# Attention latents in alternating PSUM banks, and an output projection of seven block products

## Chip, core and metric

One core of a Trainium2 chip runs the kernel. The metric is device time in microseconds (us), lower is better. Five engines run side by side, each with its own queue in order: TensorE (PE; its weight loads are shown as PEld), VectorE (DVE), ScalarE (ACT), GpSimd (POOL) and SyncE (SP), which issues the DMAs. Matmuls write to PSUM, in banks of 512 float32 columns; operands lie in SBUF.

## The reference

A mixer block on 2048 latent tokens of 1024 features, with 256 context tokens. Cut to what matters here:

```python
u = h @ w_in[l]                                  # h: normed, modulated x
q, k, v = _mla_qkv(u, ...)                       # 4 heads, low-rank q and kv
attn = _attend(q, k_all, v_all)                  # 2048 queries, 2304 keys
y = _branches(u, attn, w_pool[l], pool_scale[l]) @ w_out[l]
x_new = x + gate[:, None, :] * y
# _branches: concat([silu(gate_a) * attn, silu(gate_p) * pooled])
```

## The kernel before

Every float32 operand of a matmul is split into a high and a low part, and a product is three matmuls: high by high, high by low, low by high. `split` (lines 96 to 100) copies the high part on ScalarE and subtracts on VectorE (or GpSimd).

**Attention.** There are 16 blocks (4 heads by 4 groups of 512 queries), each of two halves p of 256 queries. `scores(p, i)` computes 128 queries by 2304 keys in five chunks: four of 512 columns in banks "A" (5 of them) and one of 256 in a bank "X" (2 of them); VectorE takes the maxima, ScalarE the exponentials (line 795) and VectorE transposes 32x32 blocks (line 798). `shuffle(p)` issues 16 DMAs on SP that bring the blocks into place. `pv(p)` then works in nine steps: a step makes the high half on ScalarE (line 855) and the low half on GpSimd, or for one step on VectorE (line 857), and six products (line 823) sum into the block's bank "O", of which there is one. The steps of `pv` follow the scores at some 28 score steps' distance, written out in `attn`.

At a block's end `norm` transposes the sums' reciprocals in a bank X, `latents` splits bank O into two SBUF tiles, and `finish`, called at the fourth step of the next half, multiplies these by the value weights (line 912, in a bank X), by the gate (line 914) and stores to `brd`. The gate is multiplied by the reciprocals on GpSimd before (line 895). The last half, `pv_last`, transposes on TensorE (line 841) instead of by DMA; the order at the end is 28, 29, 31, 30.

**Output projection.** `load_wo` loads w_out in four pieces of 256 rows after the shuffles of p = 28, 29, 30 and at the end; `out_weights` splits them (lines 933 and 935) at the steps that WO_AT lists. Then for each of eight pairs of token tiles (t2): 8 x 256 columns of `brd` are loaded (line 1028), split, and multiplied in four banks of 24 products each (2 token tiles by 2 halves of the output columns; 8 row tiles by 3). VectorE multiplies each bank by the gate (line 1060), GpSimd adds x (line 1063; VectorE in the last token tile), and SP stores. The last bank is computed in two halves of 256 columns.

The scheduler of the framework orders the instructions of each engine by program order and by when their operands and buffers are free; `order(a, b)` adds an edge, and buffers of a tag ("B": 8, "M": 6, "T": 10, "W": 5) are handed out as they come free.

Of the kernel before, what the change touches and what calls it, by code (L numbers as in the profile page):

```python
# [17 lines left out]
H = 4  # L18
# [41 lines left out]
WO_AT = (1, 5, 11, 12, 12, 12, 13, 13)  # L60
# [5 lines left out]
def tile_hybrid_block(ctx: ExitStack, tc: tile.TileContext, x, c, cx, c_ctx, w_mod, b_mod, norm_g,  # L66
# [23 lines left out]
    def pt(tag, cols=512):  # L90
        return ps.tile([128, cols], F32, tag=tag, bufs=PBUFS[tag], name=nm("p" + tag))
# [346 lines left out]
    def tok(hf, k):  # L438
# [112 lines left out]
        tk = ps.tile([128, H, 128], F16, tag="X", bufs=PBUFS["X"], name=nm("pX"))  # L551
# [251 lines left out]
    PT, pool_last = {}, []  # L803
# [15 lines left out]
    def pv_mm(p, o, j2, t):  # L819
        for jj in range(2):  # L820
            j = 2 * j2 + jj
            for m, (a, c) in enumerate(((0, 0), (1, 0), (0, 1))):
                nc.tensor.matmul(o, lhsT=V[0][:, j, a], rhs=t[:, c, jj], start=(j == 0 and m == 0),  # L823
                                 stop=(j == NJ - 1 and m == 2))
# [22 lines left out]
    def pv(p):  # L847
        o = out_bank(p)
        src = PT.pop(p).rearrange("p q i j b -> p (q i) j b")
        ts = []  # L850

        def halves(j2):
            t = st("M", [2, 2, 8, 32], F16)
            s2 = src[:, :, 2 * j2:2 * j2 + 2, :].rearrange("p x j b -> p j x b")
            nc.scalar.activation(out=t[:, 0], in_=s2, func=AF.Copy)  # L855
            eng = nc.vector if j2 == 4 or (p == NP - 2 and j2 % 2) else nc.gpsimd
            lo = eng.tensor_tensor(out=t[:, 1], in0=s2, in1=t[:, 0], op=ALU.subtract)  # L857
            if eng is nc.gpsimd:
                pool_last.append(lo.ins)
            ts.append(t)  # L860

        for j2 in range(NJ // 2):
            if j2 == 0:
                halves(0)
                halves(1)
            if j2 + 2 < NJ // 2:
                halves(j2 + 2)
            t = ts.pop(0)
            pv_mm(p, o, j2, t)
            yield  # L870

    def norm(n):
# [6 lines left out]
        b = pt("X")  # L879
# [21 lines left out]
    def latents(n):  # L901

        o = O.pop(n)
        ol = [st("T", [512], F32R) for _ in range(2)]
        split(o, *ol)
        return ol

    def finish(n, ol, gau):
        h, qb = blocks[n]
        b = pt("X")  # L910
        for m, (a, c) in enumerate(((0, 0), (1, 0), (0, 1))):
            nc.tensor.matmul(b, lhsT=wuv[0][:, a, h * 128:(h + 1) * 128], rhs=ol[c], start=(m == 0), stop=(m == 2))  # L912
# [6 lines left out]
    wo = []  # L919

    wraw, tail = [], []

    def load_wo(k2):
        raw = st("B", [2, D])
        nc.sync.dma_start(out=raw, in_=w_out[k2 * 256:(k2 + 1) * 256, :].rearrange("(k p) n -> p k n", p=128))
        wraw.append(raw)

    def out_weights():
        for raw in wraw:
            w = st("W", [2, 2, D], F32R)  # L930
            wo.append(w)
            for k in range(2):
                a = nc.scalar.activation(out=w[:, 0, k], in_=raw[:, k], func=AF.Copy)
                order(tail[-1], a.ins, "the last block of attention comes first")
                nc.vector.tensor_tensor(out=w[:, 1, k], in0=raw[:, k], in1=w[:, 0, k].bitcast(F32), op=ALU.subtract)
                yield

    def pv_all():
# [11 lines left out]
        gr_ = norm(NP // 2 - 1)  # L950
        for k, _ in enumerate(pv_last(NP - 1)):
            if k == 3:
                finish(NP // 2 - 2, ol, gate_norm(*gaus))
            yield
        gau = gate_norm(*gr_)
        yield from pv(NP - 2)
        finish(NP // 2 - 1, latents(NP // 2 - 1), gau)

    PER = 10
    WO_PF = (28, 29, 30)  # L960
    pg = pv_all()

    def attn():

        done = 0
        for p in range(NP):
# [12 lines left out]
            if p == NP - 1:  # L979
                load_wo(3)  # L980
                return
            with tc.issue_after(shuffle(p)):
                if h < H and p % 8 in K_PF:
                    load_k(h, (K_PF.index(p % 8),))
                if p in WO_PF:
                    load_wo(WO_PF.index(p))

# [27 lines left out]
    ow = out_weights()  # L1015
    for n, _ in enumerate(pg):
        for _ in range(WO_AT.count(n)):
            next(ow)
    for _ in ow:
# [3 lines left out]
    gb = st("M", [D])  # L1023
    nc.sync.dma_start(out=gb, in_=gated.partition_broadcast(128))
    for t2 in range(8):
        t0 = t2 * HB
        br = st("B", [8, HB])
        nc.sync.dma_start(out=br, in_=brd[:, :, :, t0:t0 + HB].rearrange("a h p n -> p (a h) n"))
        bh, bl = st("B", [8, HB], F32R), st("B", [8, HB], F32R)
        split(br, bh, bl)  # L1030
        bank = {}

        def mm(k, n, ks, c0=0, c1=512):
            if (k, n, c0) not in bank:
                bank[k, n, c0] = pt("A")
            for kt in ks:
                w = wo[kt // 2]
                for m, (a, c) in enumerate(((bh, 0), (bh, 1), (bl, 0))):
                    nc.tensor.matmul(bank[k, n, c0][:, 0:c1 - c0], lhsT=a[:, kt, k * 128:(k + 1) * 128],  # L1039
                                     rhs=w[:, c, kt % 2, n * 512 + c0:n * 512 + c1],  # L1040
                                     start=(kt == 0 and m == 0), stop=(kt == 7 and m == 2))

        for ks in [range(8)] if t2 else [(2 * i, 2 * i + 1) for i in range(4)]:
            for k in range(2):
                for n in range(2):
                    if t2 == 7 and k == 1 and n == 1:
                        mm(k, n, ks, 0, 256)
                        mm(k, n, ks, 256, 512)
                    else:
                        mm(k, n, ks)  # L1050
        for k in range(2):
            xr = st("M", [D])
            rows = slice(t0 + k * 128, t0 + (k + 1) * 128)
            nc.sync.dma_start(out=xr, in_=x[rows, :])
            last = t2 == 7 and k == 1
            for n in range(2):
                for c0, c1 in ((0, 256), (256, 512)) if last and n == 1 else ((0, 512),):
                    nsl = slice(n * 512 + c0, n * 512 + c1)
                    o = st("T", [512])
                    nc.vector.tensor_tensor(out=o[:, 0:c1 - c0], in0=bank[k, n, c0][:, 0:c1 - c0], in1=gb[:, nsl],  # L1060
                                            op=ALU.mult)
                    eng = nc.vector if last else nc.gpsimd
                    eng.tensor_tensor(out=xr[:, nsl], in0=o[:, 0:c1 - c0], in1=xr[:, nsl], op=ALU.add)  # L1063
                    if last:
                        nc.sync.dma_start(out=out[rows, nsl], in_=xr[:, nsl])
            if not last:
                nc.sync.dma_start(out=out[rows, :], in_=xr)
# [48 lines left out]
```

## Time and profile before

| | us |
|---|---|
| median of 3 runs | 1268.37 (1267.26 to 1270.73) |
| profiled execution | 1265.99 |
| span of the profiled execution | 1264.2 |
| TensorE busy | 1208.2 (96%) |
| VectorE busy | 832.2 (66%) |
| ScalarE busy | 733.5 (58%) |
| GpSimd busy | 565.7 (45%) |

Busy time is the sum of an engine's instructions in the profile; matmuls overlap, so their durations are longer than the distance from one to the next. A line number is that of the kernel before. "Idle before, releaser" tells how long an engine stood before an instruction and which instruction of which engine ended that.

### The profile page before, as it was taken

The page shows a single profiled execution, that of the slowest core. Times are in us where ns is not written, and L with a number is a line of the kernel's source. Part 1 is how long each engine was busy: PE and PEld are TensorE (multiplying, and loading weights), DVE is VectorE, ACT ScalarE, POOL GpSimd, SP SyncE. Part 2 cuts the span into 40 slices and gives each one's busy share as a digit, 9 for nine tenths or more (in the row PEclk, how much of TensorE's full clock was granted, in tenths as well). Part 3 has the DMA queues.
Part 4 walks back from the last instruction along what each step waited for, and adds up shares of the span by engine and source line. Part 5 has one row for each costly group of instructions (what it writes and reads, how often), then busy time and mean ns, then how long its engine had stood idle before and what let it go on. Part 6 is the DMA issues. An engine that isn't in the chain of part 4 may idle for free.

```text
span 1264.2 us, 22297 instructions
## 1 busy us (share of the span) xinstructions
PE 1208.2 (96%) x7805; PEld 949.8 (75%) x7805; DVE 832.2 (66%) x1595; ACT 733.5 (58%) x1780; POOL 565.7 (45%) x638
## 2 busy tenths in 40 slices
PE   6899999999999999899999999999999999999998
PEld 2698989989899999665666566666665666788887
DVE  4876654756556555579888888888888876732211
ACT  5585655645675654367777777777777777510000
POOL 3645313525344343024566656555655574342221
PEclk9799999999999999999999999999999999999999
DMA  9546942485336646457897788878877888664321
GB/s 305 150 130 139 231 124 70 123 189 176 88 81 143 164 111 169 124 129 179 220 221 174 176 207 202 190 178 212 196 177 178 187 198 245 201 219 145 118 83 50
DMA packets 208213, 208.66 MB, mean 165 GB/s; under 512 B 92339, under 2 KB 168420, under 8 KB 207974
## 3 DMA queue, kind: packets, MB, share of 16 engines
q1 hardware_dynamic: 208102, 207.25, 63.3%
q8 instruction: 61, 1.00, 0.3%
q14 instruction: 50, 0.41, 0.1%
HBM read 98.50 MB, written 35.56 MB: 106 GB/s over the span
## 4 chain that ended last, share of the span: by engine, by line
PE 75%; DMA 9%; DVE 6%; ACT 5%; SPq 3%; issue 2%; POOL 1%; ACTq 0%; DVEq 0%; POOLq 0%
PE pA L590 17%; PE pA L774 17%; PE pA L1039 13%; PE pO L823 10%; PE pA L246 6%; DMA W<-W 2%; PE pA L521 2%; PE pX L774 2%; ACT T L795 2%; DVE W L798 2%; DMA M<-in_w_in_dram 2%; SPq L813 1%; PE pX L912 1%; DVE mx L777 1%; DMA qrd<-U 1%
## 5 line engine op out<-in xcount | busy, mean ns | idle before, releaser
L857 POOL TENSOR_TENSOR M<-W,M 128x512 f16<-128x512 f32 x244 | 291.5, 1219 | 239.1 <-ACT M L855 187.7
L590 PE MATMUL pA<-W,B 128*128 128x256 f32 x2304 | 306.4, 286 | 0.1
L774 PE MATMUL pA<-B,M 128*128 128x512 f16 x1280 | 298.1, 379 | 8.5 <-ACT T L795 6.1
L590 PEld LDWEIGHTS pA<-W,B 128*128 128x128 f32 x2304 | 289.2, 191 | 3.5 <-issue 0.9
L774 PEld LDWEIGHTS <-M 128*128 128x128 f16 x1600 | 154.7, 98 | 153.3 <-issue 13.9
L798 DVE STREAM_TRANSPOSE W<-T 128x512 f32<-128x512 f32 x310 | 194.1, 643 | 58.5 <-ACT T L795 44.6
L855 ACT ACTIVATE M<-W 128x512 f16<-128x512 f32 x279 | 162.2, 633 | 107.6 <-PE pO L823 95.0
L823 PE MATMUL pO<-M,B 128*128 128x256 f16 x1728 | 219.7, 273 | 3.0 <-POOL M L857 1.8
L823 PEld LDWEIGHTS <-B 128*128 128x128 f16 x1728 | 167.6, 98 | 48.1 <-issue 11.2
L795 ACT ACTIVATE T<-pA,nm,gm 128x512 f32<-128x512 f32 x248 | 189.3, 773 | 7.8 <-DVE nm L783 6.3
L1039 PE MATMUL pA<-W,B 128*128 128x512 f32 (+1 forms) x792 | 177.8, 384 | 1.7 <-ACT B L98 1.7
L777 DVE TENSOR_REDUCE mx<-pA 128x1 f32<-128x512 f32 x256 | 168.3, 671 | 11.5 <-PE pA L774 11.2
L1039 PEld LDWEIGHTS pA<-W,B 128*128 128x128 f32 x792 | 144.7, 188 | 30.8 <-ACT B L98 1.9
L1063 POOL TENSOR_TENSOR M<-T,M 128x512 f32<-128x512 f32 x30 | 40.7, 1361 | 110.9 <-DVE T L1060 106.7
L1060 DVE TENSOR_TENSOR T<-pA,M 128x512 f32<-128x512 f32 (+1 forms) x33 | 22.0, 672 | 100.6 <-PE pA L1039 100.6
L246 PE MATMUL pA<-B,W 128*128 128x448 f32 (+1 forms) x288 | 86.6, 372 | 0.0
L98 ACT ACTIVATE B<-M 128x1024 fp32r<-128x1024 f32 (+2 forms) x53 | 55.2, 1043 | 43.3 <-DMA M<-in_w_in_dram 37.4
L99 DVE TENSOR_TENSOR B<-M,B 128x1024 fp32r<-128x1024 f32 x48 | 59.8, 1247 | 30.9 <-ACT B L98 30.9
L98 ACT ACTIVATE B<-B 128x2048 fp32r<-128x2048 f32 x8 | 15.3, 1914 | 77.4 <-DMA B<-brd 77.4
L246 PEld LDWEIGHTS pA<-B,W 128*128 128x128 f32 x288 | 54.7, 197 | 4.4 <-DVE T L275 0.9
L246 PE MATMUL pA<-W,W 128*128 128x448 f32 (+1 forms) x144 | 52.9, 369 | 0.0
L795 ACT ACTIVATION_READ_ACCUMULATOR T<-pA,nm,gm 128x1 f32 x248 | 49.5, 200 | 0.0
(193 smaller groups left out, 1500.8 us busy)
## 6 DMA issues: line engine op xcount, KB each, us to landing
W<-W SPq DMA_DIRECT2D x496, 144.0 KB
M<-in_w_in_dram SPq DMA_DIRECT2D x48, 512.0 KB
B<-in_x_dram SPq DMA_DIRECT2D x16, 512.0 KB
B<-brd SPq DMA_DIRECT2D x8, 1024.0 KB
M<-in_x_dram SPq DMA_DIRECT2D x16, 512.0 KB
out_dram<-M SPq DMA_DIRECT2D x15, 512.0 KB
brd<-T SPq DMA_DIRECT2D x24, 256.0 KB
kd<-T SPq DMA_DIRECT2D x36, 128.0 KB
```

The lines of the kernel that those rows point to most:

```text
L98: a = nc.scalar.activation(out=hi, in_=src, func=AF.Copy)
L99: (eng or nc.vector).tensor_tensor(out=lo, in0=src, in1=hi if hi.dtype == F16 else hi.bitcast(F32), op=ALU.subtract)
L246: nc.tensor.matmul(p[:, c0:NTOK], lhsT=a[:, kt, k * 128:(k + 1) * 128], rhs=b, start=(kt == 0 and n == 0), stop=(kt == KT - 1 and n == 2))
L590: nc.tensor.matmul(p[:, i * HB:(i + 1) * HB], lhsT=w[:, a, kt, :], rhs=b[:, kt, :], start=(m == 0), stop=(m == 23))
L774: nc.tensor.matmul(b[:, s0:s0 + sn], lhsT=q[:, a, c, p % 2, i], rhs=kt[ki][:, kc, o:o + sn], start=(m == 0), stop=(m == 4))
L777: nc.vector.reduce_max(mx[:, n:n + 1], b[:, :w], axis=AX.X)
L795: nc.scalar.activation(out=e[:, :w], in_=sp[n][:, :w], func=AF.Exp, bias=ng, scale=escale, accum_out=rs[:, n:n + 1])
L798: nc.vector.transpose(TP[p][:, :, i, j0:j1, :].rearrange("p q j b -> p j q b"), e[:, :w].rearrange("p (j q b) -> p j q b", q=4, b=32))
L823: nc.tensor.matmul(o, lhsT=V[0][:, j, a], rhs=t[:, c, jj], start=(j == 0 and m == 0), stop=(j == NJ - 1 and m == 2))
L855: nc.scalar.activation(out=t[:, 0], in_=s2, func=AF.Copy)
L857: lo = eng.tensor_tensor(out=t[:, 1], in0=s2, in1=t[:, 0], op=ALU.subtract)
L1039: nc.tensor.matmul(bank[k, n, c0][:, 0:c1 - c0], lhsT=a[:, kt, k * 128:(k + 1) * 128], rhs=w[:, c, kt % 2, n * 512 + c0:n * 512 + c1], sta ...
```

## The change

**Banks.** A block's products go to bank O for even blocks and to a bank X for odd ones; `norm` uses the other of the two. `finish` writes its product into the bank that `latents` has just read, and an edge puts it behind the products of the next block that stand before it in the program.

**Projection.** Token tiles are taken in pairs as before. For the first pair (t2 = 0) four banks are computed from eight block products (`plain_pair`), each of 128 tokens by 512 features by 512 columns. For the other seven, the 2x2 blocks A (tokens by features) and B (features by columns) are multiplied by the form of Strassen and Winograd with seven block products, with sums S1 to S4 of the blocks of A, and T1 to T4 of the blocks of B. The sums are made on VectorE before the operands are split. The products are summed on VectorE as they leave PSUM, and the gate and x are applied on GpSimd in two operations (on VectorE for the last block). The second pair (t2 = 1) takes its products in another order, those without T1 to T4 first.

**Loads.** w_out is loaded in four blocks of 512 rows by 512 columns, after the shuffles of p = 26 to 29; the first pair's `brd` and x are loaded after that of p = 30, and the gate before the last steps of attention. WO_AT is spread over more steps.

The core of the diff:

```diff
-WO_AT = (1, 5, 11, 12, 12, 12, 13, 13)
+WO_AT = (1, 4, 7, 10, 13, 15, 17, 18)
+BR_AT = 16
@@ out_bank, norm, finish
-            O[p // 2] = pt("O")
+            O[p // 2] = pt("OX"[p // 2 % 2])
-        b = pt("X")
+        b = pt("XO"[n % 2])
     def finish(n, ol, gau):
-        b = pt("X")
+        ol, b = ol
         for m, (a, c) in enumerate(((0, 0), (1, 0), (0, 1))):
+            i = nc.tensor.matmul(b, lhsT=wuv[0][:, a, h * 128:(h + 1) * 128], rhs=ol[c], ...)
+            order(pv_done[-1], i.ins, "products of the next block come first")
@@ weights
+    def wo_sums():
+        def wo_sum(out, a, b, op):
+            for k in (0, 2):
+                i = nc.vector.tensor_tensor(out=out[:, k:k + 2], in0=a[:, k:k + 2], in1=b[:, k:k + 2], op=op)
+                order(op_last[3], i.ins, "the first operands come first")
+        b00, b01, b10, b11 = (wraw.pop((a, b)) for a in range(2) for b in range(2))
+        t1, t2 = st("B", [4, 512]), st("B", [4, 512])
+        wo_sum(t1, b01, b00, ALU.subtract)
+        wo_sum(b01, b11, b01, ALU.subtract)
+        yield
+        wo_sum(t2, b01, b00, ALU.add)
+        yield from wo_pair("T2", t2, "W")
+        wo_sum(t2, b10, t2, ALU.subtract)
+        yield from wo_pair("T1", t1, "B")
+        yield from wo_pair("T3", b01, "B")
+        yield from wo_pair("T4", t2, "W")
@@ projection
+    FORM = ((1, "A00", "B00"), (6, "S2", "T2"), (5, "S1", "T1"), (7, "S3", "T3"), (2, "A01", "B10"),
+            (3, "S4", "B11"), (4, "A11", "T4"))
+    def close(t2, xr, k, n, o, c0=0, c1=512, ops=(ALU.mult, ALU.add)):
+        last = t2 == 7 and (k, n) == (1, 0)
+        eng = nc.vector if last else nc.gpsimd
+        ...
+    def products(b, c, w, first, last_, c0=0, c1=512, kts=range(4)):
+        for kt in kts:
+            for m, (x0, x1) in enumerate(((0, 0), (0, 1), (1, 0))):
+                nc.tensor.matmul(b[:, c0:c1], lhsT=c[:, x0, kt, :], rhs=w[x1][:, kt, c0:c1], ...)
+    def operand(src):
+        c = st("M", [2, 4, 128], F32R)
+        nc.scalar.activation(out=c[:, 0], in_=src, func=AF.Copy)
+        op_last.append(nc.vector.tensor_tensor(out=c[:, 1], in0=src, in1=c[:, 0].bitcast(F32), op=ALU.subtract).ins)
+        return c
+    def sums_of(br):
+        for key, a, b, op in (("S1", "A10", "A11", ALU.add), ("S2", "S1", "A00", ALU.subtract),
+                              ("S3", "A00", "A10", ALU.subtract), ("S4", "A01", "S2", ALU.subtract)):
+            ...
+            nc.vector.tensor_tensor(out=v[key], in0=v[a], in1=v[b], op=op)
+    def out_pair(t2, v, xr, early={}):
+        for i, a, b in (FORM if t2 > 1 else [FORM[j] for j in (0, 4, 5, 1, 2, 3, 6)]):
+            c = early.pop(a, None) or operand(v[a])
+            pb = pt("A")
+            products(pb, c, wo[b], True, True, ...)      # 12 matmuls
+            if i == 1:
+                p1 = st("T", [512])
+                nc.scalar.copy(out=p1, in_=pb)
+            elif i == 6:
+                u = add(pb, p1)                          # VectorE, PSUM + SBUF
+            elif i == 5:
+                z = add(pb, u)
+            elif i == 7:
+                close(t2, xr, 1, 1, add(pb, z))
+                y = add(pb, u)
+            ...
@@ order of the projection
+    sums = wo_sums()
+    for n, _ in enumerate(first):                        # plain_pair(0), eight steps
+        if n == 0:
+            br, xr = load_pair(1)
+        if n < 3:
+            next(sums, None)
+        elif n == 3:
+            early["A00"], early["A01"] = (operand(blocks_of(br)[key]) for key in ("A00", "A01"))
+            v = sums_of(br)
+        elif n == 5:
+            early["S4"] = operand(v["S4"])
+        else:
+            next(sums, None)
+    for _ in sums:
+        pass
+    for t2 in range(1, 8):
+        for n, _ in enumerate(out_pair(t2, v, xr, early)):
+            if n == 1 and t2 < 7:
+                br, nxr = load_pair(t2 + 1)
+            if n == 3 and t2 < 7:
+                nv = sums_of(br)
```

## Rows read from the trace of the kernel before

**Rows 1.** The page: busy us, share of the span and instructions of each engine.
```profile
PE 1208.2 (96%) x7805; PEld 949.8 (75%) x7805; DVE 832.2 (66%) x1595; ACT 733.5 (58%) x1780; POOL 565.7 (45%) x638
```

**Rows 2.** Stretches: length, busy PE, PEld, DVE, ACT, POOL, clock, DMA share, GB/s.
```profile
556.00:1050.00 494.00, 477.27 (x3083) 302.58 (x3083) 413.71 (x849) 365.95 (x865) 295.13 (x247) 1.00 0.79 191
...
1066.00:1070.00 4.00, 3.09 (x21) 2.23 (x22) 3.93 (x8) 4.00 (x8) 0.00 (x0) 1.00 1.01 408
...
174.00:179.00 5.00, 2.92 (x22) 2.41 (x21) 4.21 (x8) 2.76 (x6) 0.52 (x1) 1.00 0.00 0
179.00:183.00 4.00, 4.00 (x19) 3.62 (x18) 1.90 (x5) 1.67 (x4) 0.19 (x1) 0.57 0.33 77
```

**Rows 3.** TensorE's waits, 340 to 1050 us: releaser, us, times, longest.
```profile
PE pX L912 <- ACT T L98: 9.0, 13, 0.7
```

**Rows 4.** Timeline at block changes (start, us, engine, line, instruction): TensorE, GpSimd.
```profile
634.28 0.73 PE L912 MATMUL pX<-T,M 128*128 128x512 f32 x2 [0.69 <-ACT T L98]
...
869.65 0.82 PE L823 MATMUL pO<-M,B 128*128 128x256 f16 x6
871.16 0.73 PE L912 MATMUL pX<-T,M 128*128 128x512 f32 x2 [0.69 <-ACT T L98]
871.88 1.69 PE L823 MATMUL pO<-M,B 128*128 128x256 f16 x14
...
868.27 4.58 POOL L857 TENSOR_TENSOR M<-W,M 128x512 f16<-128x512 f32 x4 [3.20 <-DMA W<-W]
```

**Rows 5.** Timeline of the scores' fifth chunk: products on TensorE, exponentials on ScalarE.
```profile
844.57 0.71 PE L774 MATMUL pX<-B,M 128*128 128x256 f16 x5
...
847.73 0.70 PE L774 MATMUL pX<-B,M 128*128 128x256 f16 x5 [0.15 <-DVE rr L882]
...
850.27 0.57 ACT L795 ACTIVATE T<-pX,nm,gm 128x256 f32<-128x256 f32 x1
...
855.14 0.63 ACT L855 ACTIVATE M<-W 128x512 f16<-128x512 f32 x1 [1.71 <-PE pO L823]
...
858.69 0.57 ACT L795 ACTIVATE T<-pX,nm,gm 128x256 f32<-128x256 f32 x1
```

**Rows 6.** Timeline before the projection's first products: ScalarE and TensorE.
```profile
1073.93 1.91 ACT L98 ACTIVATE B<-B 128x2048 fp32r<-128x2048 f32 x1 [3.02 <-DMA B<-brd]
...
1075.90 1.21 PE L1039 MATMUL pA<-W,B 128*128 128x512 f32 x4 [1.65 <-ACT B L98]
```

**Rows 7.** VectorE's groups by form, 1060 to 1264: busy us, mean ns | idle.
```profile
L935 DVE TENSOR_TENSOR W<-B,W 128x1024 fp32r<-128x1024 f32 x8 | 12.7, 1632 | 0.1
L99 DVE TENSOR_TENSOR M<-pA,M 128x512 f16<-128x512 f32 x9 | 5.8, 683 | 0.1
L857 DVE TENSOR_TENSOR M<-W,M 128x512 f16<-128x512 f32 x5 | 4.2, 875 | 0.0
...
L1063 DVE TENSOR_TENSOR M<-T,M 128x512 f32<-128x512 f32 x1 | 0.7, 692 | 0.1
```

**Rows 8.** Lines 935, 1063 (duration ns min/median/max), then the timeline of GpSimd and VectorE.
```profile
L935 DVE TENSOR_TENSOR W<-B,W x8: 1212/1221/2612, 1066.3 to 1088.3; 128x1024 fp32r<-128x1024 f32 x8
...
L1063 POOL TENSOR_TENSOR M<-T,M x30: 1285/1292/3342, 1108.4 to 1249.8; 128x512 f32<-128x512 f32 x30
...
1081.91 4.25 POOL L857 TENSOR_TENSOR M<-W,M 128x512 f16<-128x512 f32 x2
...
1108.36 5.86 POOL L1063 TENSOR_TENSOR M<-T,M 128x512 f32<-128x512 f32 x3 [8.83 <-DVE T L1060]
...
1109.24 2.57 DVE L99 TENSOR_TENSOR B<-B,B 128x2048 fp32r<-128x2048 f32 x1
```

**Rows 9.** Timeline of the last evacuations of banks on VectorE.
```profile
1249.07 0.69 DVE L1060 TENSOR_TENSOR T<-pA,M 128x512 f32<-128x512 f32 x1 [4.75 <-PE pA L1039]
...
1254.51 0.69 DVE L1060 TENSOR_TENSOR T<-pA,M 128x512 f32<-128x512 f32 x1 [4.75 <-PE pA L1039]
...
1260.26 0.42 DVE L1060 TENSOR_TENSOR T<-pA,M 128x256 f32<-128x256 f32 x1 [2.06 <-PE pA L1039]
```

More of the change, by code (lines that the diff above doesn't have):

```diff
@@ L917, in finish @@
         nc.sync.dma_start(out=brd[0, h, :, qb * 512:(qb + 1) * 512], in_=br)
[L919 to L926, printed above, removed]
-    def out_weights():
[L929 to L936, printed above, removed]
+    wo, wraw, tail = {}, {}, []
@@ new lines, in load_wo, with wo_pair @@
+    def load_wo(a, b):
+        raw = st("B", [4, 512])
+        nc.sync.dma_start(out=raw, in_=w_out[a * 512:(a + 1) * 512, b * 512:(b + 1) * 512]
+                          .rearrange("(k p) n -> p k n", p=128))
+        wraw[a, b] = raw
+    def wo_pair(key, raw, tag):
+        if tag == "W":
+            w = st("W", [2, 4, 512], F32R)
+            wo[key] = (w[:, 0], w[:, 1])
+        else:
+            wo[key] = (st("B", [4, 512], F32R), st("B", [4, 512], F32R))
+        hi, lo = wo[key]
+        for k in (0, 2):
+            a = nc.scalar.activation(out=hi[:, k:k + 2], in_=raw[:, k:k + 2], func=AF.Copy)
+            order(tail[-1], a.ins, "the last block of attention comes first")
+            nc.vector.tensor_tensor(out=lo[:, k:k + 2], in0=raw[:, k:k + 2], in1=hi[:, k:k + 2].bitcast(F32),
+                                    op=ALU.subtract)
+            yield
@@ new lines, in blocks_of, with plain_pair @@
+    def blocks_of(br):
+        return {f"A{m}{k}": br[:, 4 * k:4 * k + 4, m * 128:(m + 1) * 128] for m in range(2) for k in range(2)}
+    def plain_pair(t2, br, xr):
+        v = blocks_of(br)
+        c = {key: operand(v[key]) for key in ("A00", "A10", "A01", "A11")}
+        bank = {}
+        yield
+        for a in range(2):
+            for n in range(2):
+                for m in range(2):
+                    if a == 0:
+                        bank[m, n] = pt("A")
+                    products(bank[m, n], c[f"A{m}{a}"], wo[f"B{a}{n}"], a == 0, a == 1)
+                    yield
+                    if a:
+                        o = st("T", [512])
+                        nc.vector.tensor_tensor(out=o, in0=bank[m, n], in1=g[n], op=ALU.mult)
+                        close(t2, xr, m, n, o, ops=(ALU.add,))
@@ L1015, in tile_hybrid_block @@
     ow = out_weights()
+    gb = st("M", [D])
+    nc.sync.dma_start(out=gb, in_=gated.partition_broadcast(128))
+    g = [gb[:, 0:512], gb[:, 512:1024]]
     for n, _ in enumerate(pg):
@@ L1018, in tile_hybrid_block @@
             next(ow)
+        if n == BR_AT:
+            first = plain_pair(0, *pairs.pop())
+            next(first)
     for _ in ow:
         pass
[L1023 to L1067, printed above, removed]
```

79 lines of the change are left out of this document (64 added, 15 removed).

## Prediction

> **What bounds the kernel now.** I read the page's busy times first: TensorE is busy for 96% of the span, VectorE for 66%, GpSimd for 45% [rows 1]. An average over stages can mislead, so the stages come next [rows 2]. In the attention (556 to 1050 us) TensorE is busy for 477 of 494 us at a granted clock of 1.00, VectorE for 414. TensorE is the bound there, and every idle piece of it lengthens the run. The output projection, line 1039, is bound by TensorE as well: two neighbouring banks are taken out at 1249.07 and 1254.51 [rows 9], and a bank is 24 products, so a 512-column product costs 5.44 / 24 = 0.227 us. Only around 1066 does this change: VectorE is busy for 3.93 of 4 us there and TensorE for 3.09 [rows 2].
>
> Two things can shorten the run: a TensorE wait in the attention, and the number of products behind it. What must be watched is VectorE between them.
>
> **1. The latents (lines 901 to 918).** At a block's end ScalarE and VectorE read bank O, and TensorE stands before the first product of line 912 until ScalarE's copy is there: 13 times, 9.0 us in all [rows 3]. The view of one such moment [rows 4]: six products of line 823 start at 869.65. Fourteen of them take 1.69 us at some 0.27 each, so they start every (1.69 - 0.27) / 13 = 0.109 us and a seventh could start at 870.30; what starts next is line 912, at 871.16. That is 0.86 us, or 11.2 us for 13 blocks; by the view of waits it is 9.0. The change gives the next block the other bank and puts line 912 behind its products. The next block's operands must be there: GpSimd's four subtractions run from 868.27 at 4.58 / 4 = 1.15 us each, so the first is ready at 869.4 and the next at 870.6, in time [rows 4]. Later, VectorE's line 914 waits for GpSimd's line 895 anyway, so a later line 912 costs nothing; without that cover it would cost what line 914 waits. I take **-10**, with -5 and -11 as ends.
>
> **2. Which bank.** Odd blocks now hold one of the two X banks, so the scores have one for their fifth chunk. Now both are used: the chunk of 847.73 is only released by the exponential of 858.69, 11.5 us later, while a block of four such rounds lasts (871.16 - 634.28) / 7 = 33.84 us, 8.46 a round [rows 4, 5]. But that is a chunk computed before its four others; the one of 844.57 was released at 850.84, after 6.3 us [rows 5], which fits into 8.46. I take **0**, and make the rest a rival.
>
> **3. The products.** Seven of the eight pairs of token tiles go from 8 block products to 7, each of 12 products (4 row tiles by 3): 7 x 12 = 84 fewer, 84 x 0.227 = **-19.0**. This is the only term that follows from a count.
>
> **4. Moved loads and weights.** The first branch tile (line 1028) was loaded so late that ScalarE stood 3.02 us for it, and TensorE 1.65 behind that [rows 6]. Now it is loaded after the 30th shuffle. **-1.7** (0 to -2.6, with the 0.9 us idle of 1066 to 1070 [rows 2]). The four weight loads move some two scores rounds ahead, each behind 16 shuffle issues on SP; the same bytes, and the weights are first split after the last block began, so no one waits; if they or the branch tile came late, the old 1.65 would be back. The x half of the early load must wait for a K tile to come free; behind it on SP stand the gate and rv loads, for which GpSimd waits, not TensorE. Later pairs of loads wait on SP for a slot that the stores of the pair before must free; behind them are only output stores.
>
> **5. VectorE in the first two pairs.** Here is the cost. From 1065.4, VectorE must do, in order, before the first operand that needs a weight sum (S2, T2) is ready, with 0.69 us for 512 columns and 1.22 (the median) for 1024 [rows 7, 8]: 9 splits of the last block (6.1), 5 halves (3.4), 8 weight splits (9.8), 4 operand splits, 4 evacuations, 4 for the last two latents (8.3), six half sums for T1, T3, T2 (7.3), the T2 split (2.4), two early operands, four sums and S4 (4.8), T4's sum and T1's split, which stand ahead in program order (4.9), two evacuations and S2 (2.1). Together 49.1 us: 1114.5 if nothing disturbs. The same eight weight splits took 1.632 us on average in place of 1.22 [rows 7, 8], 3.3 us more, and I add about 1 for waits on ScalarE; I put **1119**. TensorE would be there earlier. The 792 products of line 1039 (744 of 0.227, 48 halves of about 0.12) are 174.7 us; the last ends at about 1260.2 [rows 9], so all else is worth 1085.5, or 1082.5 without some 3 us idle from 1066 on (0.9 and 1.65 of them in [rows 2, 6]). Add 96 products of the plain pair (21.8) and the three products that need no sum (8.2): 1112.5. So TensorE stands about **+7**; from 0 (T4 and T1 come later in the order, GpSimd is quiet) to 14 (all four T splits come first, with stretched operations).
>
> **6. The other six pairs.** One pair is 84 x 0.227 = 19.0 us. VectorE has 4 sums, 7 operand splits and 7 evacuations, 18 x 0.69 = 12.4 us. GpSimd has 8 operations of 1.29 in place of 4, 10.3 us, and ScalarE 8 copies of about 0.6 [rows 5, 7 to 9]. Each engine alone fits. But two of them disturb each other: three GpSimd operations took 5.86 us in place of 3 x 1.29 while a 2048-column subtraction of VectorE ran for 2.57, and GpSimd's two halves of 4.25 us, beside the weight splits, should have taken 2.3 [rows 4, 8]. If VectorE's eleven operations with two SBUF inputs and GpSimd's eight exclude each other, they need 7.6 + 10.3 = 17.9 of 19.0 us. The operands are split up to four products ahead, which hides short delays. I take **+2.5**, 0 to +10.
>
> The Trainium skill (SBUF — State Buffer, section on SBUF's two separate sides) calls this an exclusive lock, which whoever comes first keeps for its whole instruction: a VectorE operation with two SBUF inputs or a GpSimd one. The trace agrees in the one place where it is clean: the three GpSimd operations lost 2.0 us of the 2.57 of the VectorE one beside them [rows 8]. By shared use instead, the pair would be bound by TensorE alone, and this term 0.
>
> **7. The end.** One more VectorE operation of 256 columns between the last product and the store: **+0.4** [rows 9].
>
> **Sum.** The profiled execution took 1265.99 us, 2.4 less than the median of 1268.37. 1266.0 - 10 - 19.0 - 1.7 + 7 + 2.5 + 0.4 = 1245.2; with the 2.4 it is **1247.5** for a median.
>
> **Rivals.**
> A, VectorE isn't late: terms 5 and 6 vanish, 1238. For it: the order of products of the second pair delays the sums' users by 8.2 us. Against: 49 us of work.
> B, VectorE is late by 14 or more and TensorE idles so long that its clock falls. The trace has such a place: TensorE idle for 2 of 5 us at 174, then a granted clock of 0.57 for 4 us [rows 2], worth 1.7 us. 1247.5 + 7 + 2 + some stretched pairs = 1259. The skill (TensorE: Matmul & The Clock Gate, the table on why this matters) also tells to avoid idle gaps; by it this falls on the same side as the row.
> C, one X bank is not enough: if ScalarE puts its 4.5 copies of a round, 0.63 us each [rows 5], between the exponentials, a round is 6.3 + 2.8 = 9.1 us, 0.65 more than 8.46, in 32 rounds: +21. That gives 1268, no change. Against: TensorE can go on with the other products meanwhile.
> D, slower: VectorE's operations with two SBUF inputs wait for GpSimd's as often as there are any. Place: the seven short pairs, and the list of term 5. Price: 12.4 + 10.3 = 22.7 us a pair, 3.7 x 7 = 26; and some ten GpSimd operations beside the list (halves, gates, the plain pair's sums) at about 1.2 are 12 us where I put 4. 1247.5 - 2.5 + 26 + 8 = 1279. It decides, against the median of before, from 21.2 us a pair: 1247.5 - 2.5 + 8 + 7 x 2.2 = 1268.4. For it: the 17.9 of 19.0. Against: operands are made ahead, and the seven evacuations from PSUM can run meanwhile. It is the lock of the page above, taken to its end.
> E, the change does not do what it says: the scheduler still puts line 912 where TensorE waits; 1257.5, inside the range.
>
> **Chances.** The forecast (1239 to 1256) 0.58, A 0.13, B and E together 0.14, C 0.08, D 0.07. A measurement of this kernel can tell about 0.3% from no change, 3.8 us: faster means below 1264.6. Faster 0.85, same 0.08, slower 0.07. The range reaches from A's lower end (term 1 at -11, term 4 at -2.6: 1236; I write 1235) to B with a little more than I put (1262).
>
> **What would show it.** Term 1: no TensorE wait for line 98 at the latents, and a block's period of about 33.0. Term 2: no waits of the fifth chunk for the exponentials. Term 3: 696 projection products at 0.227. Terms 4 and 5: a TensorE stop not before the first branch tile but in the second pair, with VectorE busy throughout, ended by VectorE's operand splits. Term 6: banks of 2.72 us without gaps from the third pair on, and GpSimd's operations above 1.29. I am wrong if the attention's period grows, or if the pairs are much longer than 19 us.

## The result, and the profile after

| | before | after |
|---|---|---|
| median of 4 runs (us) | 1269.55 (1267.26 to 1271.38) | 1247.97 (1246.47 to 1250.04) |
| profiled execution, its span | 1265.99, 1264.2 | 1248.26, 1246.5 |

The ratio is 0.9839 (95% interval 0.9822 to 0.9855). The forecast was 1247.5 with a range of 1235 to 1262. In the spans, the time goes like this (block starts are the first product of each block in TensorE's timeline):

| stretch | before | after | difference | predicted |
|---|---|---|---|---|
| start to block 0 of attention | 555.3 | 557.6 | +2.3 | 0 |
| block 0 to block 15 | 513.5 | 503.6 | -9.9 | -10 (terms 1, 2) |
| block 15 to the last product | 191.1 | 179.5 | -11.6 | -11.2 (terms 3 to 6) |
| last product to the end | 4.3 | 5.8 | +1.5 | +0.4 (term 7) |
| sum | 1264.2 | 1246.5 | -17.7 | -20.8 |

The first row lies ahead of everything that was changed; in the profiles of this study it runs from 555.3 to 560.2. The medians differ by 21.6.

The marks don't cut off the same work in both kernels, since the change moves products past them. Between the first products of blocks 0 and 1 stand 120 products of the scores after and 145 before, and between those of blocks 13 and 15 it is 170 and 145. A product of 512 columns takes 0.216 us (20 of line 775 below take 4.32), so 25 are 5.4 us. Behind the mark of block 15 the changed kernel has 11 small products more (8 transposes of the last half, one of `norm`, two of `finish`), by the timelines some 1.5 us. For equal work I estimate -8.4 for the second row and -13.1 for the third. From block 1 to block 13 both kernels have the same 2544 products: 406.7 us before and 398.6 after, 8.2 less.

Line numbers are now those of the changed kernel: 823 became 824, 774 and 795 became 775 and 796, 855 and 857 became 857 and 861, 912 became 916, 914 became 919, 933 and 935 became 942 and 944, 1039 became 1049, 1060 and 1063 became 1076 and 1041. New are 956 (sums of weights), 1054 and 1055 (operands of the branch tile), 1084 (sums of the tile's blocks) and 1090 (sums of the products). The rows of a run have that run's own numbers, which can be a few lines off from these.

Busy times of the page after (answers to [rows 1]): VectorE has 82 us more, TensorE 22 less.

```profile
PE 1186.4 (95%) x7709; PEld 936.6 (75%) x7709; DVE 914.2 (73%) x1706; ACT 761.6 (61%) x1840; POOL 602.7 (48%) x666
```

Stretches after (columns as in [rows 2]):

```profile
1066.00:1070.00 4.00, 4.00 (x35) 3.40 (x34) 4.00 (x7) 3.05 (x6) 0.00 (x0) 1.00 1.04 360
...
1078.00:1082.00 4.00, 2.34 (x16) 2.02 (x16) 4.00 (x3) 4.00 (x7) 3.00 (x2) 1.00 0.03 2
1082.00:1086.00 4.00, 1.74 (x7) 1.08 (x6) 4.00 (x6) 0.18 (x1) 0.00 (x0) 0.89 0.72 260
1086.00:1090.00 4.00, 4.00 (x14) 3.16 (x13) 4.00 (x6) 0.00 (x0) 0.00 (x0) 0.68 0.00 0
...
1130.00:1150.00 20.00, 20.00 (x90) 16.56 (x89) 19.43 (x22) 5.33 (x10) 17.92 (x12) 1.00 0.50 171
```

VectorE is busy for 4.00 of 4 in nearly every stretch from 1066 to 1118, and TensorE is short of work at 1058 to 1066 and at 1074 to 1086, not later. In the six later pairs TensorE never stops. VectorE is busy for 97% and GpSimd for 90% of the time in the last row; from 1130 to 1230 it is 89% and 74%.

TensorE's waits from 340 to 1050 us (answer to [rows 3]), then its timeline at the block change that [rows 4] show:

```profile
PE pA L775 <- ACT T L796: 14.1, 24, 2.3
...
PE pX L775 <- DVE rr L886: 0.2, 1, 0.2
```
```profile
862.77 0.82 PE L824 MATMUL pX<-M,B 128*128 128x256 f16 x6
863.43 4.48 PE L775 MATMUL pA<-B,M 128*128 128x512 f16 x20
867.75 0.71 PE L775 MATMUL pX<-B,M 128*128 128x256 f16 x5
868.29 2.13 PE L824 MATMUL pX<-M,B 128*128 128x256 f16 x18
870.18 0.94 PE L916 MATMUL pO<-T,M 128*128 128x512 f32 x3
```

The wait of line 912 for the latents is gone: line 916 now comes 24 products into the next block, in the other bank, with no idle time before it. But TensorE now waits for the exponentials longer, 14.1 us in place of 6.1 (from block 1 to block 13, 8.0 in place of 2.1).

TensorE's waits from 1030 us on, and its timeline at the change to the projection; then VectorE's timeline in the same place:

```profile
PE pX L824 <- DVE M L861: 2.7, 2, 1.8
PE pA L1049 <- DVE M L1055: 2.3, 1, 2.3
```
```profile
1079.66 1.25 PE L824 MATMUL pX<-M,B 128*128 128x256 f16 x10 [1.82 <-DVE M L861]
1080.67 2.09 PE L1049 MATMUL pA<-W,M 128*128 128x512 f32 x8
1085.02 8.23 PE L1049 MATMUL pA<-W,M 128*128 128x512 f32 x28 [2.26 <-DVE M L1055]
```
```profile
1075.88 2.17 DVE L944 TENSOR_TENSOR W<-B,W 128x1024 fp32r<-128x1024 f32 x1
1077.98 1.63 DVE L861 TENSOR_TENSOR M<-W,M 128x512 f16<-128x512 f32 x1
1079.53 4.83 DVE L944 TENSOR_TENSOR W<-B,W 128x1024 fp32r<-128x1024 f32 x3
1084.29 2.48 DVE L1055 TENSOR_TENSOR M<-B,M 128x512 fp32r<-128x512 f32 x4
...
1111.33 2.39 DVE L1055 TENSOR_TENSOR M<-T,M 128x512 fp32r<-128x512 f32 x2
```

TensorE stands for the last block's halves and for the first pair's operands, which stand in VectorE's queue behind weight splits of 1.2 to 2.2 us. In the second pair, where I had put the stop, VectorE is just in time: the operand of S4 is ready at 1113.1, some 0.2 us before the first product with its low half, and that of S2 at 1113.7, where its first product starts at 1115.6.

Lines 1041 and 1090 from 1118 us on (duration ns min/median/max), and VectorE's last rows (answer to [rows 9]):

```profile
L1041 POOL TENSOR_TENSOR T<-T,M x27: 1287/1674/1761, 1119.0 to 1238.9; 128x512 f32<-128x512 f32 x27
...
L1090 DVE TENSOR_TENSOR T<-pA,T x50: 415/681/693, 1118.2 to 1241.4; 128x512 f32<-128x512 f32 x48, 128x256 f32<-128x256 f32 x2
...
L1055 DVE TENSOR_TENSOR M<-T,M x18: 676/1508/1783, 1127.4 to 1225.8; 128x512 fp32r<-128x512 f32 x18
```
```profile
1241.10 0.76 DVE L1090 TENSOR_TENSOR T<-pA,T 128x256 f32<-128x256 f32 x2 [2.23 <-PE pA L1049]
...
1242.43 0.75 DVE L1041 TENSOR_TENSOR B<-T,B 128x256 f32<-128x256 f32 x2
```

GpSimd's operations and VectorE's with two SBUF inputs stretch each other (1.29 to 1.67, 0.68 to 1.51 in the median); VectorE's with one input from PSUM do not (0.68).

### The profile page after: what moved, and what is told of

Read it like the earlier page. It is cut to its first block, busy times and chain, and to the rows that moved or that the text cites. A ratio compares the mean times of both kernels' runs of the same rounds, so it can differ in the third digit from the quotient of the medians.

```text
span 1246.5 us, 22420 instructions
## 1 busy us (share of the span) xinstructions
PE 1186.4 (95%) x7709; PEld 936.6 (75%) x7709; DVE 914.2 (73%) x1706; ACT 761.6 (61%) x1840; POOL 602.7 (48%) x666
## 4 chain that ended last, share of the span: by engine, by line
PE 79%; DMA 7%; ACT 5%; DVE 5%; SPq 2%; issue 2%; POOL 1%; DVEq 0%; ACTq 0%; POOLq 0%
PE pA L775 20%; PE pA L591 18%; PE pA L1049 12%; PE pA L247 6%; PE pO L824 5%; PE pX L824 5%; PE pA L522 3%; PE pX L775 2%; ACT T L796 2%; DMA M<-in_w_in_dram 2%; ACT M L857 2%; SPq L814 2%; PE pA L497 1%; DMA qrd<-U 1%; DMA B<-in_w_mod_dram 1%
## 5 line engine op out<-in xcount | busy, mean ns | idle before, releaser
L861 POOL TENSOR_TENSOR M<-W,M 128x512 f16<-128x512 f32 x244 | 277.5, 1158 | 249.1 <-ACT M L857 219.0
L775 PE MATMUL pA<-B,M 128*128 128x512 f16 x1280 | 299.5, 379 | 17.0 <-ACT T L796 14.1
L591 PEld LDWEIGHTS pA<-W,B 128*128 128x128 f32 x2304 | 290.2, 192 | 3.5 <-issue 0.9
L778 DVE TENSOR_REDUCE mx<-pA 128x1 f32<-128x512 f32 x256 | 169.3, 672 | 11.2 <-PE pA L775 10.6
L1049 PE MATMUL pA<-W,M 128*128 128x512 f32 (+1 forms) x528 | 120.9, 388 | 2.3 <-DVE M L1055 2.3
L824 PE MATMUL pO<-M,B 128*128 128x256 f16 x864 | 112.8, 273 | 3.8 <-POOL M L861 1.9
L824 PE MATMUL pX<-M,B 128*128 128x256 f16 x864 | 111.1, 273 | 5.3 <-DVE M L861 2.7
L1049 PEld LDWEIGHTS pA<-W,M 128*128 128x128 f32 x528 | 98.6, 190 | 22.8 <-DVE M L1055 2.7
L100 DVE TENSOR_TENSOR B<-M,B 128x1024 fp32r<-128x1024 f32 x48 | 61.6, 1285 | 33.0 <-ACT B L99 32.8
L1041 POOL TENSOR_TENSOR B<-T,B 128x512 f32<-128x512 f32 x31 | 50.2, 1621 | 29.5 <-DVE T L1076 27.6
L1041 POOL TENSOR_TENSOR T<-T,M 128x512 f32<-128x512 f32 x27 | 43.0, 1593 | 38.4 <-DVE T L1090 27.8
L1054 ACT ACTIVATE M<-B 128x512 fp32r<-128x512 f32 x32 | 19.7, 628 | 51.6 <-PE pA L1049 39.1
```

The source lines that it names most:

```text
L100: (eng or nc.vector).tensor_tensor(out=lo, in0=src, in1=hi if hi.dtype == F16 else hi.bitcast(F32), op=ALU.subtract)
L591: nc.tensor.matmul(p[:, i * HB:(i + 1) * HB], lhsT=w[:, a, kt, :], rhs=b[:, kt, :], start=(m == 0), stop=(m == 23))
L775: nc.tensor.matmul(b[:, s0:s0 + sn], lhsT=q[:, a, c, p % 2, i], rhs=kt[ki][:, kc, o:o + sn], start=(m == 0), stop=(m == 4))
L778: nc.vector.reduce_max(mx[:, n:n + 1], b[:, :w], axis=AX.X)
L824: i = nc.tensor.matmul(o, lhsT=V[0][:, j, a], rhs=t[:, c, jj], start=(j == 0 and m == 0), stop=(j == NJ - 1 and m == 2))
L1041: eng.tensor_tensor(out=o[:, c0:c1] if op == ALU.mult else xr[:, k, n, c0:c1], in0=o[:, c0:c1], in1=a[:, c0:c1], op=op)
```

## The experiments

The kernel before had medians of 1269.02 to 1269.82 beside these runs. Once more unaltered, the changed kernel took 1248.14 (expectation: 

> The changed kernel once more, unaltered, beside the other three on one chip: 1247 to 1249 by all theories.

).

**The banks alone, and without the edge.** The kernel before with the diff's part "Banks" (`out_bank`, `norm`, `finish` with its edge). With it goes an edit that the section on the change doesn't name: the last block's `norm` and its gate come later, `norm` inside the last half's products. The second run lacks the edge:

```diff
-            order(pv_done[-1], i.ins, "products of the next block come first")
```


> The kernel before with the change of banks alone: blocks alternate between bank O and a bank X, line 912 writes into the bank just read and stands behind the next block's products; the projection stays as it was. Theory (the two parts add, and the bank part is worth the block period 33.84 -> 33.15 us): 13 x 0.7 = 9 us less, about 1260.5. Rival (the wait only goes over to the exponentials, whose waits in the changed kernel went from 6.1 to 14.1 us): 1267 to 1270.

> The same as e1_banks without the edge that puts line 912 behind the next block's products. Theory (the edge is needed: the product now writes into a bank that VectorE still reads, so placed early it waits for ScalarE and VectorE): at most half of the gain, 1265 to 1270. Rival (the second bank alone frees TensorE, the order of line 912 does not matter): the same as e1_banks, 1260.5.

Measured: 1267.42, ratio 0.9983 (0.9972 to 0.9995), and 1271.83, 1.0017 (1.0006 to 1.0029). The second is above both expectations. Without the edge there is no gain: a block's period (blocks 2 to 12) is 33.76 us, where it is 33.84 before and 33.16 with the edge. TensorE no longer waits for the latents, but in their place for halves and for the norm's operand, by its waits from 340 to 1050 us in that run:

```profile
PE pO L823 <- POOL M L857: 3.7, 7, 0.9
...
PE pO L880 <- DVE nm L782: 2.7, 7, 0.4
PE pO L823 <- ACT M L855: 2.5, 2, 1.5
PE pX L823 <- POOL M L857: 2.4, 7, 0.3
```

With it, block 1 to block 13 take 397.9 us, as in the changed kernel (398.6; before, 406.7). So the time of the first run is the rival's, but not by the rival's mechanism: the gain is there, and is lost behind it. Block 13 to block 15 take 67.8 (before 61.6 with 25 products of the scores fewer, changed 65.2), and from there to the end it is 201.8 in place of 195.4, with the 1.5 us of moved products. One place where that is lost, in the trace of the banks alone: GpSimd, then VectorE, then TensorE.

```profile
1080.80 9.29 POOL L858 TENSOR_TENSOR M<-W,M 128x512 f16<-128x512 f32 x2 [20.37 <-ACT M L856]
```
```profile
1080.48 3.48 DVE L937 TENSOR_TENSOR W<-B,W 128x1024 fp32r<-128x1024 f32 x3
```
```profile
1089.03 1.44 PE L823 MATMUL pX<-M,B 128*128 128x256 f16 x6 [3.60 <-POOL M L858]
```

Two halves of 1.15 us took GpSimd 9.29, while VectorE ran weight splits back to back at full speed (3.48 for three), and behind them three halves and a split of the branch tile until 1088. In this profile the granted clock fell as well, to 0.82 and 0.75 in the two stretches from 1062 to 1070 and to 0.81 and 0.77 from 1086 to 1094. Then I put the change's spacing of the splits into that kernel:

```diff
-WO_AT = (1, 5, 11, 12, 12, 12, 13, 13)
+WO_AT = (1, 4, 7, 10, 13, 15, 17, 18)
```


> The run with the alternating banks alone (1267.42), with one line more of the change: the weight splits at steps 1, 4, 7, 10, 13, 15, 17, 18 in place of 1, 5, 11, 12, 12, 12, 13, 13. In the run with the banks alone two halves on GpSimd lasted 9.29 us beside six weight splits on VectorE one behind the other, and TensorE waited 3.6 us for them. Theory (these took back the banks' gain): with the splits spread, the end is as before, and the banks' 8 to 10 us show: 1259 to 1263. Rival (the loss at the end has another cause, such as the late tile of the first pair): 1265 to 1268.

Measured: 1262.63, 0.9946 (0.9924 to 0.9968), 4.8 less than with the banks alone, as the theory said. GpSimd's halves in the same place:

```profile
1079.79 3.65 POOL L858 TENSOR_TENSOR M<-W,M 128x512 f16<-128x512 f32 x2 [19.68 <-ACT M L856]
```

The granted clock shows 1.00 throughout here. What of the 4.8 us is the shorter halves and what the clock, no run separates.

**The projection alone.** The changed kernel with the banks as before (`finish` takes a bank X again, without the edge; the last block's `norm` stays late):

```diff
-            O[p // 2] = pt("OX"[p // 2 % 2])
+            O[p // 2] = pt("O")
-        b = pt("XO"[n % 2])
+        b = pt("X")
...
```


> The changed kernel with the change of banks undone: one bank O, line 912 into a bank X with no edge; the projection with seven products stays. Theory (19.0 for 84 products, less about 8 that TensorE loses around the last block and the first pair, less 1 to 2 at the end): 1269.5 - 10 = about 1258 to 1260. Rival (the loss around the last block comes from the banks): 1250.

Measured: 1260.2, 0.9932 (0.9911 to 0.9954). As the terms 3 to 7 say (-19.0 - 1.7 + 7 + 2.5 + 0.4 = -10.8), 9.6 us. The wait for the latents is there again, 7.6 us.

**Operands earlier, weights later.** In the changed kernel, to let TensorE begin the projection while the last block lacks halves:

```diff
-WO_AT = (1, 4, 7, 10, 13, 15, 17, 18)
-BR_AT = 16
+WO_AT = (1, 4, 7, 10, 17, 18, 18, 18)
+BR_AT = 12
-        c = {key: operand(v[key]) for key in ("A00", "A10", "A01", "A11")}
+        c = {key: operand(v[key]) for key in ("A00", "A10")}
         yield
+        c.update({key: operand(v[key]) for key in ("A01", "A11")})
```


> The changed kernel with the first two operands of the plain pair split at step 12 of the last steps in place of 16, ahead of the third and fourth weight block, which follow at steps 17 and 18; the other two operands come after the last block. Theory (TensorE loses 7.5 us from 1058 to 1086 because the operands stand behind the weights on VectorE, plus 1.6 us at the lower clock): TensorE fills these gaps, 2 to 7 us less than the changed kernel, 1241 to 1246. Rival (VectorE's list as a whole is the bound until the second pair): the wait moves to the second pair, 1247 to 1249.

Measured: 1253.31, 0.9883 (0.9862 to 0.9905): 5 us slower than the changed kernel, and above both expectations. The stop in the first pair is gone, and a longer one, 3.5 us, stands in the second. Then with the weights left where they were, so without the `WO_AT` line of that diff:

> The changed kernel with the first branch tile loaded four shuffles earlier and the operands of A00 and A10 made first, those of A01 and A11 after the last block; the weights stay where they are. Theory (VectorE's list, full from 1062 to 1118 us in the changed kernel, is the bound as a whole; S2's operand came only some 1.4 us before it was needed): what TensorE gains in the last block it loses again in the second pair, 1245.5 to 1248. Rival (the stops around 1075 to 1086 come from the order alone): 5 us or more are gained, 1241 to 1243.

Measured: 1254.59, 0.9876 (0.9852 to 0.9901). Both theories were too low. TensorE in the second pair, the stretches with its clock, and VectorE and ScalarE ahead of it:

```profile
1111.15 0.80 PE L1049 MATMUL pA<-B,M 128*128 128x512 f32 x1 [3.95 <-DVE B L944]
1114.52 0.80 PE L1049 MATMUL pA<-B,M 128*128 128x512 f32 x1 [2.57 <-ACT B L942]
```
```profile
1110.00:1114.00 4.00, 0.80 (x1) 0.29 (x1) 4.00 (x3) 0.59 (x1) 2.22 (x2) 0.50 0.35 131
1114.00:1118.00 4.00, 3.48 (x8) 2.61 (x9) 4.00 (x5) 1.41 (x2) 2.74 (x2) 0.50 0.56 177
```
```profile
1080.33 0.69 DVE L861 TENSOR_TENSOR M<-W,M 128x512 f16<-128x512 f32 x1 [4.03 <-ACT M L857]
```
```profile
1079.66 0.63 ACT L857 ACTIVATE M<-W 128x512 f16<-128x512 f32 x1 [3.51 <-PE pX L824]
```

The early products push the last block's products back. ScalarE's halves wait for these, VectorE's for ScalarE's: VectorE, full in the changed kernel, stands for 4.03 us here, and its last weight split ends at 1122.5 (1118.3 in the changed kernel). TensorE meets it in the second pair, and its granted clock falls to 0.50, the lower level. So the stop isn't moved away by the order of the operands. That VectorE's list as a whole is the bound from 1062 to about 1118 is not shown by these two runs; the next one, and the two plain pairs below, bear on it.

**VectorE's list shorter.** The kernel of the first of these two runs without the eight sums of weights:

```diff
-        wo_sum(t1, b01, b00, ALU.subtract)
-        wo_sum(b01, b11, b01, ALU.subtract)
...
-        wo_sum(t2, b01, b00, ALU.add)
-        yield from wo_pair("T2", t2, "W")
+        yield from wo_pair("T2", b00, "W")
...
```

The sums of weights are left out of the result, so it is not the reference's.

> As the run with the operands of A00 and A10 first and the last weight blocks late, but without the eight half sums of weights (their places in the products are taken by single blocks of w_out, so the sums of weights are left out of what is computed). That run stood 3.5 us in its second pair before an operand of VectorE and fell into a lower clock behind it. Theory (VectorE's list in the first two pairs is the bound there): eight operations of about 1.15 us, 9 us, leave the list, the stop in the second pair goes with its slow stretch: 5 to 8 us less than that run, 1246 to 1248. Rival (the stop comes from the order of the operands by the edges, not from the amount of work): the stop stays, 1251 to 1254.

Measured: 1246.2, 0.9819 (0.98 to 0.9837), 7.1 us less for some 9 us of VectorE's work, as the theory said; TensorE's only wait in the second pair is 0.68 us. The edit also takes away two tiles of the tag "B" (`t1`, `t2`), and no run tells what those are worth.

**VectorE's work on GpSimd.**

```diff
-            nc.vector.tensor_tensor(out=lo[:, k:k + 2], ...)
+            eng = nc.gpsimd if key in ("B10", "B11") else nc.vector
+            eng.tensor_tensor(out=lo[:, k:k + 2], ...)
```


> The changed kernel with four of the eight low parts of the weights (1024 columns each, blocks B10 and B11) on GpSimd in place of VectorE, in stretches where GpSimd is idle in the changed kernel (1057 to 1070, 1081 to 1104). VectorE's list becomes 4 x 1.22 = 4.9 us shorter; each operation on GpSimd should take 2 x 1.29 = 2.6 us. Theory 1 (operations of two SBUF inputs on VectorE and on GpSimd exclude each other): the 10.3 us of GpSimd hold VectorE up for more than the 4.9 it is spared, so the time is the same or up to 5 us longer, 1248 to 1253. Theory 2 (the two share, and mostly overlap): TensorE's stops around 1082 become shorter, 1243 to 1245.

Measured: 1251.48, 0.9859 (0.9841 to 0.9877), 3.5 us more than the changed kernel. VectorE, then GpSimd, then TensorE:

```profile
1080.55 6.00 DVE L1056 TENSOR_TENSOR M<-B,M 128x512 fp32r<-128x512 f32 x3 [1.45 <-ACT M L1055]
1089.01 2.71 DVE L1056 TENSOR_TENSOR M<-B,M 128x512 fp32r<-128x512 f32 x1 [2.45 <-ACT M L1055]
```
```profile
1075.67 2.87 POOL L945 TENSOR_TENSOR W<-B,W 128x1024 fp32r<-128x1024 f32 x1 [2.23 <-ACT W L942]
1078.50 1.60 POOL L861 TENSOR_TENSOR M<-W,M 128x512 f16<-128x512 f32 x1
...
1085.97 5.20 POOL L945 TENSOR_TENSOR W<-B,W 128x1024 fp32r<-128x1024 f32 x2
```
```profile
1080.16 1.47 PE L824 MATMUL pX<-M,B 128*128 128x256 f16 x12 [2.85 <-POOL M L861]
```

Four operand splits took 8.7 us where 4 x 0.68 is 2.7: VectorE lost 6.0 and was spared 4.9. But TensorE's longest stop here, 2.85 us, ends with a half of GpSimd that stood behind a weight split in GpSimd's own queue. The time is as theory 1 said; what of the 3.5 us is the contention and what that queue, this run doesn't separate.

**More work for GpSimd.** In the pairs from the third on:

```diff
+        if t2 > 1 and not last:
+            nc.gpsimd.tensor_tensor(out=junk[:, 0:512], in0=o[:, 0:512], in1=g[n], op=ALU.mult)
```


> The changed kernel with one more GpSimd operation per result bank in the pairs from the third on (a gate product into a tile that nobody reads; the result stays as it is): 12 instead of 8 GpSimd operations a pair. If VectorE's 11 operations of two SBUF inputs (7.6 us) and GpSimd's 12 of 1.29 (15.5 us) exclude each other, a pair needs 23.1 us in place of its 19.0, and the six pairs give up to +24: 1265 to 1272. If they only stretch each other at the expense of slack, GpSimd has 15.5 of 19.0 us of work and TensorE stays the bound: 1247 to 1250, with GpSimd's and VectorE's two-input operations longer in the median than 1.62 and 1.04 us.

Measured: 1256.25, 0.9896 (0.9877 to 0.9915), 8.3 us more, between the two. GpSimd and VectorE in the fifth pair, and GpSimd's last row:

```profile
1177.44 1.84 POOL L1044 TENSOR_TENSOR junk<-T,M 128x512 bf16<-128x512 f32 x1
1179.24 1.75 POOL L1041 TENSOR_TENSOR B<-T,B 128x512 f32<-128x512 f32 x1
1180.96 1.74 POOL L1044 TENSOR_TENSOR junk<-T,M 128x512 bf16<-128x512 f32 x1
```
```profile
1178.16 1.67 DVE L1086 TENSOR_TENSOR T<-T,B 128x512 f32<-128x512 f32 x1
1179.75 1.80 DVE L1086 TENSOR_TENSOR B<-B 128x512 f32<-128x512 f32 x1
1181.47 1.78 DVE L1086 TENSOR_TENSOR T<-B,T 128x512 f32<-128x512 f32 x1
```
```profile
1251.76 1.26 POOL L1044 TENSOR_TENSOR junk<-T,M 128x512 bf16<-128x512 f32 x1
```

Where both queues are full, one operation of each takes about 1.74 us together, less than the 0.68 + 1.29 = 1.97 of turns and more than the 1.29 of sharing. (VectorE's operations alone start 0.60 us apart, as at 1099.09 and 1099.69 in the changed kernel, so turns would rather take 1.89.) By this estimate a pair costs GpSimd 12 x 1.29 + 11 x (1.74 - 1.29) = 20.4 us, 1.4 over TensorE's 19.0, and six pairs 8.6: about what was measured. TensorE is not touched by it: the last product starts at 1241.28 (1240.72 in the changed kernel). GpSimd's arrears come out behind it, and its last operation ends at 1253.

**Two plain pairs.** Early operands as above, and the second pair from eight block products too; then the second pair alone, which completes a square:

```diff
+        if n == 3:
+            second = plain_pair(1, br, xr)
+            next(second)
+    for n, _ in enumerate(second):
+        if n == 1:
+            br, xr = load_pair(2)
+        if n == 5:
+            v = sums_of(br)
+        next(sums, None)
...
-    for t2 in range(1, 8):
+    for t2 in range(2, 8):
...
```

The operands that the changed kernel makes ahead for its second pair go with this edit.

> The second pair too is computed from eight block products, and the form of seven begins with the third; the branch tile of the first pair is loaded after the 26th shuffle and its first two operands are made first. This costs 12 products of 0.227 us (2.7) and gives VectorE a whole pair (21.8 us) more until the sums of weights are needed. Theory (VectorE's list is late for the last block and the first pair): some 7 us of TensorE's stops go for 2.7 us of products, 1242 to 1245. Rival (the stops come from what must be done before the first pair whatever follows: halves, splits of the last block and weights): they stay, 1249 to 1252.

> The changed kernel with the second pair computed from eight block products as well, and the first pair's tile and operands as in the changed kernel. It is the fourth corner of a square: the run with both edits gave 1245.05, the changed kernel 1247.97. Theory: the second plain pair only gives room behind the first pair, and TensorE's stops stand before that, so by itself it costs its products, 2.7 us: 1249.5 to 1251.5; it pays only together with the early operands. Rival (it relieves VectorE at once, since the sums come later): 1244 to 1247.

| | one plain pair | two |
|---|---|---|
| operands as in the change | 1247.97, 1248.14 | 1251.56 |
| operands early | 1254.59 | 1245.05 |

The ratios of the second column are 0.9849 (0.9834 to 0.9863) and 0.9805 (0.9783 to 0.9828); both times lie just above the upper end of what their theories said. Each edit alone costs 3.5 or 6.5 us; the two together give 3. With both, TensorE stands neither in the first pair nor in the second, though VectorE has idle time there (a stretch, then TensorE's timeline):

```profile
1078.00:1082.00 4.00, 4.00 (x22) 2.95 (x21) 0.98 (x1) 0.63 (x1) 1.16 (x1) 1.00 0.00 0
```
```profile
1098.89 30.11 PE L1049 MATMUL pA<-W,M 128*128 128x512 f32 x132
```

This version has the lowest median of those that compute the reference; its interval overlaps that of the changed kernel a little, and the two were not timed side by side.

## Why the prediction was right, and where it was not

**Term 1** (-10): -9.9 by the marks, and about -8.4 for equal work; that the first so nearly meets the forecast is luck. Block 0 is 5.3 us shorter and the last two blocks are 3.6 longer, but these are mostly the 25 products of the scores (5.4 us) that moved from one to the other. The gain is in the twelve periods between, 8.2 us: a period is 33.16 in place of 33.84, where about 33.0 was forecast. In them the latents' wait of 8.3 us went entirely, and the wait for the exponentials grew from 2.1 to 8.0. All waits listed there fell by 3.8 us (12.6 to 8.8) and the time by 8.2, so the attention's time isn't the sum of these waits. **Rival E** (line 916 still stands where TensorE waits) did not come; but the run without the edge shows that the wait can go and almost nothing be won (33.76 in place of 33.84 a period), since others follow it.

**Term 2** (0) and **rival C**: the fifth chunk waits 0.2 us in all. The longer waits are those of the four other chunks' banks. Right.

**Term 3** (-19.0): 696 products, and from 1093 us on without a gap. Right.

**Terms 4 to 6**: -1.7 + 7 + 2.5 = +7.8, measured -11.6 + 19.0 = +7.4 by the marks and about -13.1 + 19.0 = +5.9 for equal work. The sum was near and the place wrong. The step that failed is the one that put all of VectorE's work ahead of the S2 operand in one list and asked when TensorE comes to its end. I let the 1.65 us before the first products vanish [rows 6], and never asked when the first pair's own operands are ready. They too stand in VectorE's queue, behind weight splits; so TensorE lost its time there (1.8 and 2.3 us, and smaller pieces), which made it late for the second pair, where the list was then just ready. The two runs with early operands show the other side of it: there the stop is in the second pair. In the one with late weights VectorE's operand split ends it (3.5 us), as I had described it; in the other a weight split of VectorE and a weight copy of ScalarE do (3.95 and 2.57).

**Term 6** (+2.5): 0. The stretching is there, and TensorE doesn't feel it. The list that counts is that of VectorE's operations with two SBUF inputs and GpSimd's, 7.6 + 10.3 = 17.9 of 19.0 us as forecast, and the seven sums from PSUM lie beside it. The Trainium skill (SBUF — State Buffer, section on SBUF's two separate sides) has an exclusive lock for a whole instruction. The trace agrees on who disturbs whom, and that operations from PSUM are left alone; on the size it differs a little: 1.74 us for a turn of both, not 1.97, or 1.89 by the distance of VectorE's starts. **Rival D** took this to its end, and failed at the step that added the evacuations to the locked work (22.7 where 17.9 counts). The run with 12 operations shows where its kind of case begins: above 19.0 us, and then behind the last product.

**Rival A** (VectorE isn't late) is refuted by the stretches above. **Rival B** (a stop long enough to lower the clock) came true for a moment: 0.89 and 0.68 around 1086, eight products 0.2 us late each, 1.6 us.

**Term 7** (+0.4): +1.5. From the last product's start to VectorE's end it is 1.2 more (2.5 in place of 1.3), and behind that 0.3. Both halves of the last product's columns now lie in one bank, and VectorE takes both out only behind the last product (two operations at 1241.10, idle for 2.23 us before). In the kernel before each half had a bank of its own, and the first was taken out at 1257.31, ahead of the last at 1260.26 [rows 9]. So six operations of a half stand behind the last product, where I had counted three.

**The parts together.** The banks gave 2.3 us alone, the projection 9.6, both 21.6. Of the 9.7 between, 4.8 came back with the spacing of the weight splits, which the change brings along with the projection (with the lower clock of that one profile in it). In the profiles, from block 0 to the end, the banks with the spacing give 6.1, the projection alone 10.9, both 20.0. Of the 3.0 between, 2.6 lie between blocks 13 and 15 (67.8 us with banks and spacing, 65.2 in the changed kernel). The first has a stop of 2.06 us there that the second lacks, behind a half of ScalarE that stood 5.5 us, by the profile for a DMA of `norm`'s reciprocals. Which part of the change takes it away stays open.

## What to carry to other kernels

Before an engine is given new work, list what it does in the stretch where the work falls, in its order, and check every product that waits for that list, the first one too: the stop stands where the list first runs behind, not where its longest part ends. Here another order only moved the stop; it went when the bound engine got less work or more time. Before a time is compared between two marks, count that the same work lies between them. Two changes in one commit can need each other: test the square of both before one of them is called useless.

## What the hardware showed that I had not expected

Which of two engines loses by the contention is not fixed. In the kernel with the banks alone VectorE's splits ran at full speed (3.48 us for three) and two GpSimd halves took 9.29 us in place of 2.3; with the fuller GpSimd the two took turns, from 1130 to 1240 us at a loss of 41.8 us for VectorE (81.9 us for 59 operations of 0.68) and 24.8 for GpSimd (109.9 us for 66 of 1.29).

The same stop doesn't always lower the clock. In the changed kernel it fell after the stops of 1.82 and 2.26 us, to 0.89 and 0.68 in one profile and to 0.75 and 0.83 in the other. In the run with more work for GpSimd, with the same two stops, it shows 1.00, and so it does in the run with the second plain pair alone:

```profile
1082.00:1086.00 4.00, 1.74 (x8) 1.12 (x7) 4.00 (x6) 0.20 (x1) 0.00 (x0) 1.00 0.78 262
1086.00:1090.00 4.00, 4.00 (x20) 3.26 (x19) 4.00 (x6) 0.04 (x1) 0.00 (x0) 1.00 0.00 0
```
